# A convolution layer whose weights are split on GpSimd, with its filler products in three reduced-precision parts

## The chip, the cores and the metric

The kernel runs on one core of one Trainium2 chip. The time is the device time of one execution in microseconds (us); it counts as the median over runs. Five engines work beside each other, each through its own fixed list of instructions: TensorE (PE in the profile; its weight loads are PEld), VectorE (DVE), ScalarE (ACT), GpSimd (POOL) and SyncE (SP), which here starts the loads from memory.

## The reference

One step of a trunk of two layers with d = 1024 is computed for 384 columns (tokens): 128 of a sample group (8 streams of 16 tokens) and 256 of a prompt. Each layer has a half-step SwiGLU, a mixer, a cross-attention into 256 memory tokens and another half-step SwiGLU. The mixer of layer 0 is the convolution module that the change is about, the mixer of layer 1 a gated DeltaNet.

```python
def conformer_conv_module(h, conv_buf, w_in, b_in, dw, dw_b, ln_g, ln_b, w_out, b_out):
    u = h @ w_in + b_in
    val, gate = jnp.split(u, 2, axis=-1)
    u = val * jax.nn.sigmoid(gate)
    hist = jnp.concatenate([conv_buf.astype(u.dtype), u], axis=1)
    c = causal_depthwise_conv(hist, dw) + dw_b
    c = jax.nn.silu(layer_norm(c, ln_g, ln_b))
    return c @ w_out + b_out, hist[:, -(CONV_W - 1):]
```

`dw` has 31 taps. Apart from the trunk's output, the keys and values of the prompt's memory are outputs too: for each layer, 256 memory rows times a 1024x1024 matrix for the keys and one for the values. They depend on nothing but the inputs, so they can be computed at any time before layer l's cross-attention uses them.

## The kernel before

**Products.** An fp32 matrix product is made from three products in the faster format fp32r: each operand is split into a high part (a cast, ACT, L189) and a low part (the difference, L197), and high times high, high times low and low times high are added up in PSUM. A weight chunk is 128 rows by 1024 columns. `get` (L276) loads it into one of three buffers `raw`, casts it to `whi` and subtracts into `wlo`; both have eight buffers. In the kernel before, all subtractions are VectorE's. `proj` (L725) gets a chunk and multiplies it with the 384 columns of activations `hTh`, `hTl` (24 matmuls). Loads are started by SyncE, stores by GpSimd (L273), and each of these waits in its place in its engine's list.

**Order.** An `Emitter` records all operations, and a `Scheduler` (L304) sorts them once, ahead of time, into one fixed list per engine, on costs that the code states for each operation. The chip doesn't reorder them.

**The convolution stage** (`conv`, L965). The 1024 features are 8 tiles. For each tile c there are two projections (chunks `cg`, `cv`), the gate (`glu`: a sigmoid on ACT, two multiplications on VectorE, stores of the new history on GpSimd), and 31 taps on VectorE (L210: one multiply-add with both inputs in SBUF for each tap; `TENSOR_SCALAR`, L204, for the first). Fifteen of them for the sample tokens are done earlier, in `old_taps` (L946). Tiles are tapped two at a time. Then, over all tiles: the mean of the features by matmuls with a constant matrix `onesd`, the layer norm `ln` for each of three token tiles, and the output product with eight chunks `co`, token tile by token tile (`tokenwise`). It can start on a token tile when its layer norm is done.

**Filler.** The memory's keys and values are 32 pieces (2 layers, 4 heads, keys and values, 2 halves). `kv` (L903) makes a piece with 16 true fp32 matmuls of 128 columns, each of which the profile records as two. The table `KV` says at which place of the program how many pieces are offered to TensorE: 20 of them in the convolution's stage, between the projections and the mean, while VectorE is at the taps. Whatever is left when a cross-attention needs it is made ahead of it.

**GpSimd before.** It makes small statistics of the norms (`stat`, 128x1 to 128x6), some copies in DeltaNet, memsets and all stores. In the convolution's stage it has memsets and stores.

Of the kernel before, what the change touches and what calls it, by code (L numbers as in the profile page):

```python
# [8 lines left out]
F32 = mybir.dt.float32  # L9
F32R = mybir.dt.float32r  # L10
AF = mybir.ActivationFunctionType
ALU = mybir.AluOpType
# [39 lines left out]

# columns of the per-feature table
# [5 lines left out]
# constant matrices: causal blocks, block sums, decay masks, block-doubling masks  # L59
# [8 lines left out]
def chunk_names():  # L68
    names = [("mem", 0), ("mem", 1), ("bout",)]
    for l in range(2):  # L70
        for i in range(2):
            for f in range(FF):
                names += [("g", l, i, f), ("u", l, i, f), ("d", l, i, f)]
            names += [(n, l, i, j) for n in ("g4", "u4") for j in range(4)]
        names += [("q4", l, 0, j) for j in range(4)]
        for k in range(KT):
            names += [("wq", l, k), ("wo", l, k), ("wk", l, k // 2, k % 2), ("wv", l, k // 2, k % 2)]
# [16 lines left out]
class Emitter:  # L94
    """Records the program in issue order. Tasks beside the main stream are advanced by running
    clocks of the engines, so that their matmuls fall where their operands are ready."""
# [153 lines left out]
    def quad(self, mms):  # L250
        """Products into four groups of 32 rows, which the tensor engine works on at once."""
# [24 lines left out]
    def get(self, name, dest=None):  # L276
        """The two parts of a weight chunk: loaded and split as early as their room is free."""
# [9 lines left out]
        self.tt(lo, raw, hi.bitcast(F32), ALU.subtract)  # L287
# [16 lines left out]
class Scheduler:  # L304
    """Orders the recorded program: a list schedule by the longest way to the end, on the engines'
    known costs, that keeps every dependence between the operations."""
# [8 lines left out]
    def cell(self, ap):  # L315
        """(what, bits): the tile and the columns in it that an operand covers."""
# [123 lines left out]
class Region:  # L440
    """First-fit allocation of the columns of one tile."""
# [5 lines left out]
    def take(self, n, keep=0, high=False):  # L447
# [13 lines left out]
        # of the places at an edge of a hole, the one whose columns were freed the longest ago  # L461
# [19 lines left out]
class Model:  # L481
    def __init__(self, nc, tc, A, O, s, ps):
# [41 lines left out]
    def alloc(self, n, keep=0):  # L524
        """(columns, handle) for the main stream."""
# [19 lines left out]
    def _bank(self):  # L545
# [3 lines left out]
        # the one that has been free for longest  # L549
# [38 lines left out]
    def rows(self, kind, i):  # L588
        """A row of gains on all partitions."""
# [4 lines left out]
    def rstd(self, s1, s2, dep):  # L594
        """(s1 + s2) ** -0.5."""
# [6 lines left out]
    def chain(self, t, y, yb, gpost, gpre, half=False, cross=False):  # L602
        """x += post(y); the next sublayer's normalized input, transposed and split."""
# [79 lines left out]
    def first_chunks(self, names, chains, split):  # L683
# [12 lines left out]
        res = []  # L696
# [1093 lines left out]
```

## Time and profile before

| | |
|---|---|
| median of 3 runs | 1893.7 us (1892.61 to 1894.55) |
| span of the profiled execution | 1891.9 us, 1.8 us below that median |
| projections of the convolution on TensorE, fp32 pieces between them | 312.6 to 397 us |
| fp32 pieces alone | 397 to 454 us |
| taps (after `old_taps`) | 324.2 to 454.2 us |
| mean and layer norm | 454.2 to 477 us |
| first matmul of the output product | 477.0 us |

The profile is one execution. A row such as `L197 DVE TENSOR_TENSOR wlo<-raw,whi 128x1024 fp32r<-128x1024 f32 x361 | 438.1, 1221 | 570.7 <-ACT whi L189 542.7` reads: line 197, engine VectorE, the operation, its output and inputs with their shape, 361 times; 438.1 us busy in all, 1221 ns each; VectorE was idle for 570.7 us just ahead of these, most of it waiting for ACT's cast of line 189. In the timeline a row has its start and its length, both in us. A row of windows has the stretch, its length, and the busy time and number of instructions of each engine.

### The profile page before, as it was taken

To read this page: it belongs to the slowest core of one execution; us is meant where nothing else is said; L and a number is where in the kernel's file an instruction comes from. 1 tells how busy PE (TensorE), PEld (TensorE's weight loads), DVE (VectorE), ACT (ScalarE), POOL (GpSimd) and SP (SyncE) were. 2 spreads that over 40 slices of the span, in tenths; PEclk is the share of its full clock that TensorE was granted. 3 is DMA by queue.
4 is the path that set the end of the run, shared out by engine and by line. 5 is a ranking of instruction groups with operands and counts; after the bars stand their busy time and mean duration, and the time that the engine had idled before them with its cause. 6 is when DMAs were issued, how large, how long until landed. Compare 5 with 4: busy or idle time off the path is not lost.

```text
span 1891.9 us, 27912 instructions
## 1 busy us (share of the span) xinstructions
PE 1870.6 (99%) x10863; PEld 1682.6 (89%) x10863; DVE 1025.5 (54%) x1940; ACT 794.5 (42%) x1589; POOL 168.8 (9%) x407
## 2 busy tenths in 40 slices
PE   8999999999999999999999999999999999999998
PEld 7999999999877899999899999989898767899997
DVE  6564436998653633334633344788886734533333
ACT  4333334312643533233433233787786533433332
POOL 1000002111100100000100000323321101000000
PEclk9999999999999999999999999999999999999999
DMA  8544434556685443434533343433324782444431
GB/s 300 179 136 125 134 112 121 128 147 216 219 312 210 156 129 128 134 123 130 163 122 117 120 134 101 128 97 99 123 90 124 236 311 101 134 134 134 122 123 45
DMA packets 88469, 278.83 MB, mean 147 GB/s; under 512 B 18001, under 2 KB 20561, under 8 KB 88337
## 3 DMA queue, kind: packets, MB, share of 16 engines
q1 hardware_dynamic: 86080, 271.42, 44.7%
q0 software_dynamic: 2256, 5.64, 0.9%
q8 instruction: 85, 1.39, 0.3%
q14 instruction: 48, 0.39, 0.1%
HBM read 265.09 MB, written 11.92 MB: 146 GB/s over the span
## 4 chain that ended last, share of the span: by engine, by line
PE 97%; ACT 1%; DMA 1%; DVE 0%; POOL 0%; issue 0%; SPq 0%; DVEq 0%; POOLq 0%; ACTq 0%
PE ps L247 91%; PE ps L266 3%; PE ps L259 2%; DMA raw<-in_w 0%; POOL stat L197 0%; ACT big L190 0%; DMA x<-in_x 0%; DVE big L210 0%; ACT whi L189 0%; SPq L270 0%; ACT big L189 0%; ACT hTl L190 0%; ACT L190 0%; DVE big L197 0%; DVE wlo L197 0%
## 5 line engine op out<-in xcount | busy, mean ns | idle before, releaser
L197 DVE TENSOR_TENSOR wlo<-raw,whi 128x1024 fp32r<-128x1024 f32 x361 | 438.1, 1221 | 570.7 <-ACT whi L189 542.7
L189 ACT CAST whi<-raw 128x1024 fp32r<-128x1024 f32 x361 | 374.5, 1050 | 640.3 <-PE ps L247 584.6
L247 PE MATMUL ps<-hTh,wlo 128*128 128x384 f32 x1680 | 498.3, 341 | 0.0
L247 PE MATMUL ps<-hTl,whi 128*128 128x384 f32 x1680 | 497.1, 342 | 0.0
L247 PE MATMUL ps<-hTh,whi 128*128 128x384 f32 (+1 forms) x1680 | 496.9, 342 | 0.0
L247 PEld LDWEIGHTS ps<-hTl,whi 128*128 128x128 f32 x1680 | 308.9, 188 | 8.0 <-issue 2.1
L247 PEld LDWEIGHTS ps<-hTh,whi 128*128 128x128 f32 x1680 | 308.8, 188 | 7.9 <-issue 1.2
L247 PE MATMUL ps<-big 128*128 128x128 f32 (+5 forms) x1944 | 308.0, 288 | 7.1 <-DMA big<-in_w 6.7
L247 PEld LDWEIGHTS ps<-hTh,wlo 128*128 128x128 f32 x1680 | 308.7, 188 | 6.5 <-issue 2.3
L247 PEld LDWEIGHTS ps<-big 128*128 128x128 f32 (+1 forms) x1944 | 269.6, 190 | 40.3 <-issue 20.8
L247 PE MATMUL ps<-whi,rbh 128*128 128x512 f32 x672 | 206.0, 396 | 0.4 <-ACT big L189 0.4
L247 PE MATMUL ps<-wlo,rbh 128*128 128x512 f32 x672 | 203.8, 395 | 0.0
L247 PE MATMUL ps<-whi,rbl 128*128 128x512 f32 x672 | 202.5, 393 | 0.0
L210 DVE SCALAR_TENSOR_TENSOR big<-big,cols 128x384 f32<-128x384 f32 (+13 forms) x424 | 189.5, 497 | 2.2 <-ACT big L190 0.3
L247 PEld LDWEIGHTS ps<-whi,rbl 128*128 128x128 f32 x672 | 125.7, 188 | 24.7 <-issue 0.4
L247 PEld LDWEIGHTS ps<-wlo,rbh 128*128 128x128 f32 x672 | 125.3, 188 | 24.6 <-issue 0.4
L247 PEld LDWEIGHTS ps<-whi,rbh 128*128 128x128 f32 x672 | 124.8, 188 | 21.1 <-ACT big L189 0.6
L197 DVE TENSOR_TENSOR big<-big,ps 128x64 f32<-128x64 f32 (+4 forms) x219 | 86.4, 405 | 39.8 <-PE ps L247 39.2
L266 PE MATMUL ps<-ident,big 128*128 128x128 f32 x479 | 89.5, 279 | 5.5 <-DVE big L210 5.4
L247 PE MATMUL ps<-whi,hTh 128*128 128x512 f32 x240 | 87.2, 399 | 0.7 <-ACT hTh L189 0.7
L189 ACT COPY big<-ps 32x32 f32<-32x32 f32 (+5 forms) x155 | 49.6, 324 | 90.2 <-PE ps L247 64.3
L247 PE MATMUL ps<-whi,hTl 128*128 128x512 f32 x240 | 86.3, 398 | 0.0
(82 smaller groups left out, 1350.7 us busy)
## 6 DMA issues: line engine op xcount, KB each, us to landing
raw<-in_w SPq DMA_DIRECT2D x362, 512.0 KB, 3.8
big<-in_w SPq DMA_DIRECT2D x37, 512.0 KB, 5.1
big<-in_ck SPq DMA_DIRECT2D x32, 512.0 KB, 6.5
big<-in_cv SPq DMA_DIRECT2D x32, 512.0 KB, 6.3
big<-in_npre SPq DMA_DIRECT2D x8, 512.0 KB, 7.5
out_pkv<-big POOLq DMA_DIRECT2D x32, 128.0 KB, 5.0
big<-in_npost SPq DMA_DIRECT2D x8, 512.0 KB, 7.3
big<-out_pkv SPq DMA_DIRECT2D x8, 512.0 KB, 5.1
```

What stands on the lines that cost most here:

```text
L189: return self._on("A", cost, dep, lambda: sc.copy(out, in_), [in_], w)
L197: return self._on(eng, cost, dep, lambda: e.tensor_tensor(out=out, in0=a, in1=b, op=op), [a, b], [out])
L210: lambda: v.scalar_tensor_tensor(out=out, in0=a, scalar=s, in1=b, op0=op0, op1=op1), [a, s, b], [out])
L247: self._add("P", cost, lambda: t.matmul(out, lhsT, rhs, start=start, stop=stop, **kw), [lhsT, rhs], [out])
L259: t.matmul(out, lhsT, rhs, start=start, stop=stop)
L266: self._add("P", 109.0, lambda: t.transpose(out, in_, ident), [in_, ident], [out])
```

## The change

The low parts of all weights that the convolution layer uses are made on GpSimd: `get` takes the engine as an argument. These are the sixteen projection chunks, the eight chunks of the output product, its bias, and 20 chunks of the memory products below: 45 subtractions of 128x1024.

The 20 filler pieces in the convolution become three-part products (`kv_split`): all values, as 16 chunks of 256 rows by 512 columns (192 matmuls of 512 columns), and two key pieces (48 matmuls of 256 columns). The memory itself is loaded and split for them into `rbh`, `rbl`. The other 14 key pieces stay true fp32 products in their old places, with 8 matmuls of 256 columns in place of 16 of 128; since the queue holds just the keys now, two of them are left for DeltaNet's place in the table.

The sum over features for the mean is begun on GpSimd: `total` adds the first six tiles (five additions of 128x384), and the mean takes three matmuls, of `total` and the last two tiles, in place of eight. The chunks of keys on chip at the start are 3, not 4. Comments are gone; the lines of `Emitter` keep their numbers.

```diff
-    def get(self, name, dest=None):
+    def get(self, name, dest=None, eng="V"):
...
-        self.tt(lo, raw, hi.bitcast(F32), ALU.subtract)
+        self.tt(lo, raw, hi.bitcast(F32), ALU.subtract, eng=eng)
...
-SLOTS = 4               # chunks of keys and values on chip at the start
+SLOTS = 3
...
-KV = {"start": 3, "f00": 3, "conv": 20, "co": 3, "xo": 0, "f01": 1, "f10": 2, "dn": 6, "f11": 0}
+KV = {"start": 3, "f00": 3, "conv": 2, "co": 3, "xo": 0, "f01": 1, "f10": 2, "dn": 6, "f11": 0}
...
-        self.kvq = [(k, l, h, i) for l in range(2) for h in range(XH) for k in ("wk", "wv") for i in range(2)]
+        self.kvq = [("wk", l, h, i) for l in range(2) for h in range(XH) for i in range(2)]
...
+    def kv_split(self, keys):
...
+        for i in range(2):
+            c = slice(i * D, (i + 1) * D)
+            E.get(("mem", i), dest=(mh[:, c], ml[:, c]), eng="G")
...
+        for l in range(2):
+            for u in range(2):
...
+                for q in range(4):
+                    j, wh, wl = E.get(("v4", l, u, q), eng="G")
+                    for k in range(2 * q, 2 * q + 2):
+                        s = slice(512 * (k % 2), 512 * (k % 2) + 512)
+                        for m in range(2):
+                            c = slice(m * P, (m + 1) * P)
+                            E.mm(o[m], mh[:, k, c], wh[:, s], k == 0, False)
+                            E.mm(o[m], mh[:, k, c], wl[:, s], False, False)
+                            E.mm(o[m], ml[:, k, c], wh[:, s], False, k == KT - 1)
...
+        for _ in range(keys):
...
+            _, l, h, i = self.kvq.pop()
+            j, wh, wl = E.get(("wk", l, h, i), eng="G")
+            o, b = self.bank()
+            self.gmm(o[:, 0:MEM], wh, wl, 0, MEM, mh, ml)
...
-            for m in range(2):
-                c = slice(m * P, (m + 1) * P)
-                for k in range(KT):
-                    a, b_ = (w[:, k, :], mem[:, k, c]) if kind == "wk" else (mem[:, k, c], w[:, k, :])
-                    E.mm(o[:, c], a, b_, k == 0, k == KT - 1)
+            for k in range(KT):
+                E.mm(o[:, 0:MEM], w[:, k, :], mem[:, k, :], k == 0, k == KT - 1)
...
-                    E.mm(mean[:, 0:NTOK], self.onesd, cO[:, c, :], c == 0, c == KT - 1)
...
+                if c0 == 0:
+                    E.tt(total, cO[:, 0, :], cO[:, 1, :], ALU.add, dep=e, eng="G")
+                elif c0 < KT - 2:
+                    for c in cs:
+                        E.tt(total, total, cO[:, c, :], ALU.add, dep=e, eng="G")
+                else:
+                    E.mm(mean[:, 0:NTOK], self.onesd, total, True, False)
+                    for c in cs:
+                        E.mm(mean[:, 0:NTOK], self.onesd, cO[:, c, :], False, c == KT - 1)
...
-                og, bg, eg = self.proj(("cg", c))
-                ov, bv, ev = self.proj(("cv", c))
+                og, bg, eg = self.proj(("cg", c), "G")
+                ov, bv, ev = self.proj(("cv", c), "G")
...
-        self.kv(KV["conv"])
+        self.kv_split(KV["conv"])
...
-        jb, bh, bl = E.get(("bout",), dest=bo)
+        jb, bh, bl = E.get(("bout",), dest=bo, eng="G")
...
-        held = [E.get(("co", k)) for k in range(KT)]
+        held = [E.get(("co", k), eng="G") for k in range(KT)]
```

The scheduler makes new lists of this. On GpSimd, at the taps of the middle tiles, there stood the stores of history (`pconv`, `sconv`), of memory pieces (`pkv`) and a memset:

```order
L273 DMA out_pkv<-big 128x2x128 x2
L273 DMA out_pkv<-big 128x256
L273 DMA out_pconv<-big 128x30
L236 MEMSET big 128x30
L273 DMA out_sconv<-big 1024x1x30
L273 DMA out_pkv<-big 128x256
```

Now the subtractions stand among the history's stores, and after the last of these fifteen follow one another, up to the first addition of `total`:

```order
L197 TENSOR_TENSOR wlo_82<-raw_86,whi_74 128x1024
L197 TENSOR_TENSOR wlo_83<-raw_87,whi_75 128x1024
L197 TENSOR_TENSOR wlo_84<-raw_88,whi_76 128x1024
L273 DMA out_pconv<-big 128x30 x2
L273 DMA out_sconv<-big 1024x1x30
L273 DMA out_pconv<-big 128x30
L197 TENSOR_TENSOR wlo_85<-raw_86,whi_77 128x1024
L197 TENSOR_TENSOR wlo_78<-raw_87,whi_70 128x1024
```

So three subtractions stand ahead of stores that wait for a glu, and the rest behind them. Of the 45, eight stand among the statistics of the feed-forward sublayer ahead of the convolution, and 36 after the first tap.

On VectorE, at the second and third tile's glu (the operations that read `ps`), the list before had subtractions between the taps:

```order
L210 SCALAR_TENSOR_TENSOR big_95<-big_95,cols_92 128x235
L197 TENSOR_TENSOR wlo2_80<-raw2_88,whi2_72 128x1024
L210 SCALAR_TENSOR_TENSOR big_95<-ps5_101,cols_92,big_95 128x256
L210 SCALAR_TENSOR_TENSOR big_95<-big_95,cols_92 128x236
L204 TENSOR_SCALAR big_95<-big_95,cols_92 128x256
```

In the list after, the first two tiles' glu stand close together ahead of the taps, and no subtraction between them:

```order
L210 SCALAR_TENSOR_TENSOR big_95<-ps5_101,cols_92,big_95 128x256
L210 SCALAR_TENSOR_TENSOR big_95<-ps5_101,cols_92,big_95 128x8x16
L204 TENSOR_SCALAR big_95<-big_95,cols_92 128x256
L210 SCALAR_TENSOR_TENSOR big_95<-big_95,cols_92 128x227
L210 SCALAR_TENSOR_TENSOR big_95<-big_95,cols_92 128x228
L210 SCALAR_TENSOR_TENSOR big_95<-ps7_103,cols_92,big_95 128x256
L210 SCALAR_TENSOR_TENSOR big_95<-ps7_103,cols_92,big_95 128x8x16
```

On TensorE, behind the last projection, the value chunks begin (each of `whi`, `wlo`, `rbh` and `rbl` a part of a weight or of the memory), where the fp32 pieces `ps<-big 128x128` had stood:

```order
L247 MATMUL ps6_102<-hTh_66,wlo3_81 128x384
L247 MATMUL ps7_103<-whi4_74,rbh_68 128x512
L247 MATMUL ps7_103<-wlo4_82,rbh_68 128x512
L247 MATMUL ps7_103<-whi4_74,rbl_69 128x512
L247 MATMUL ps7_103<-whi4_74,rbh_68 128x512
```

Four projections are interleaved after the first, so that 94 projection matmuls stand ahead of the end of the second tile's chunks. The mean's three matmuls stand behind all value chunks and both keys:

```order
L247 MATMUL ps7_103<-rbh_68,wlo4_82 128x256
L247 MATMUL ps4_100<-big_95 128x384 x3
L247 MATMUL ps5_101<-big_95 128x256 x8
```

More of the change, by code (lines that the diff above doesn't have):

```diff
@@ L76, in chunk_names @@
         for k in range(KT):
-            names += [("wq", l, k), ("wo", l, k), ("wk", l, k // 2, k % 2), ("wv", l, k // 2, k % 2)]
+            names += [("wq", l, k), ("wo", l, k), ("wk", l, k // 2, k % 2), ("v4", l, k // 4, k % 4)]
     for k in range(KT):
@@ L681, in dmm, with first_chunks @@
             E.pump()
-    def first_chunks(self, names, chains, split):
+    def first_chunks(self, names, chains, split, eng="V"):
         E = self.E
@@ L689, in first_chunks @@
         for n in names[:split]:
-            j, hi, lo = E.get(n)
+            j, hi, lo = E.get(n, eng=eng)
             o, b = self.bank()
@@ L700, in first_chunks @@
             res.append((o, b, e))
-        return res + [self.proj(n) for n in names[split:]]
+        return res + [self.proj(n, eng) for n in names[split:]]
     def wide(self, o, w, t):
@@ L723, in turn, with proj @@
         return o.rearrange("p (k c) -> p k c", k=4), e
-    def proj(self, name):
-        j, hi, lo = self.E.get(name)
+    def proj(self, name, eng="V"):
+        j, hi, lo = self.E.get(name, eng=eng)
         o, b = self.bank()
@@ L879, in kv_open, with result @@
         return True
+    def kv_split(self, keys):
+        E = self.E
+        vt = E.vt
+        mh, ml = (a.rearrange("p k c -> p (k c)")[:, 0:2 * D] for a in (self.rbh, self.rbl))
+        for i in range(2):
+            c = slice(i * D, (i + 1) * D)
+            E.get(("mem", i), dest=(mh[:, c], ml[:, c]), eng="G")
+        mh, ml = (a.rearrange("p (k m) -> p k m", k=KT) for a in (mh, ml))
+        res, rh = self.alloc(1024)
+        nres = [0]
+        def result(o, n):
+            r = res[:, nres[0] % 2 * 512:nres[0] % 2 * 512 + n]
+            nres[0] += 1
+            E.act(r, o[:, 0:n], dep=0)
+            return r
+        for l in range(2):
+            for u in range(2):
+                (o, b) = self.bank2()
+                for q in range(4):
[7 more added lines that the diff above has]
+                            E.mm(o[m], ml[:, k, c], wh[:, s], False, k == KT - 1)
+                            E.pump()
+                    E.done(j)
+                for m in range(2):
+                    r = result(o[m], 512)
+                    for n in range(2):
+                        E.store(self.O["pkv"][l, 2 * u + n][:, 512 + m * MEM:512 + (m + 1) * MEM],
+                                r[:, n * MEM:(n + 1) * MEM])
+                self.bfree(b)
+        for _ in range(keys):
[3 more added lines that the diff above has]
+            self.gmm(o[:, 0:MEM], wh, wl, 0, MEM, mh, ml)
+            E.done(j)
+            E.store(self.O["pkv"][l, h][:, i * MEM:(i + 1) * MEM], result(o, MEM))
+            self.bfree(b)
+        self.free(rh)
+        E.vt = vt
     def early(self, what, order):
@@ L922, in kv @@
             o, b = self.bank()
-            for m in range(2):
-                c = slice(m * P, (m + 1) * P)
-                for k in range(KT):
-                    a, b_ = (w[:, k, :], mem[:, k, c]) if kind == "wk" else (mem[:, k, c], w[:, k, :])
-                    E.mm(o[:, c], a, b_, k == 0, k == KT - 1)
+            for k in range(KT):
+                E.mm(o[:, 0:MEM], w[:, k, :], mem[:, k, :], k == 0, k == KT - 1)
             E.act(res, o[:, 0:MEM], dep=0)
             self.bfree(b)
-            dst = self.O["pkv"][l, h]
-            if kind == "wk":
-                E.store(dst[:, i * MEM:(i + 1) * MEM], res)
-            else:
-                E.store(dst[:, 512:1024].rearrange("p (m d) -> p m d", m=2)[:, :, i * P:(i + 1) * P],
-                        res.rearrange("p (m d) -> p m d", m=2))
+            E.store(self.O["pkv"][l, h][:, i * MEM:(i + 1) * MEM], res)
             if len(self.kvq) >= self.kvslots:
@@ L998, in taps @@
         def taps():
+            total, th = yield from self.galloc(NTOK)
             for c0 in range(0, KT, 2):
@@ L1021, in taps @@
                     self.free(hist[c][1], hist[c][3])
-                    E.mm(mean[:, 0:NTOK], self.onesd, cO[:, c, :], c == 0, c == KT - 1)
+                if c0 == 0:
[7 more added lines that the diff above has]
+                        E.mm(mean[:, 0:NTOK], self.onesd, cO[:, c, :], False, c == KT - 1)
+                    self.free(th)
             self.conv_end = e
@@ L1030, in conv @@
             if c == 0:
-                (og, bg, eg), (ov, bv, ev) = self.first_chunks([("cg", c), ("cv", c)], chains, SPLIT["conv"])
+                (og, bg, eg), (ov, bv, ev) = self.first_chunks([("cg", c), ("cv", c)], chains, SPLIT["conv"], "G")
             else:
-                og, bg, eg = self.proj(("cg", c))
-                ov, bv, ev = self.proj(("cv", c))
+                og, bg, eg = self.proj(("cg", c), "G")
+                ov, bv, ev = self.proj(("cv", c), "G")
             glu(c, og, bg, eg, ov, bv, ev)
@@ L1699, in pack @@
             w[i, 0] = f("ca_b_out")[0]
-        elif t in ("g4", "u4", "q4"):
-            a = wq[n[1]] if t == "q4" else (wg if t == "g4" else wu)[n[1], n[2]]
+        elif t in ("g4", "u4", "q4", "v4"):
+            if t == "v4":
+                a = wv[n[1]][:, n[2] * 512:(n[2] + 1) * 512]
+            else:
+                a = wq[n[1]] if t == "q4" else (wg if t == "g4" else wu)[n[1], n[2]]
             w[i] = a[n[3] * 256:n[3] * 256 + 256, 0:512].reshape(2, P, 512).transpose(1, 0, 2).reshape(P, D)
@@ L1709, in pack @@
             w[i] = g_type(wq[n[1]], n[2] * P)
-        elif t in ("wk", "wv"):
-            w[i] = g_type((wk if t == "wk" else wv)[n[1]], n[2] * MEM + n[3] * P)
+        elif t == "wk":
+            w[i] = g_type(wk[n[1]], n[2] * MEM + n[3] * P)
         elif t == "wo":
```

## The prediction

> **What bounds the kernel now.** The page comes first, for the shares of the engines over the whole span.
>
> ```profile
> span 1891.9 us, 27912 instructions
> PE 1870.6 (99%) x10863; PEld 1682.6 (89%) x10863; DVE 1025.5 (54%) x1940; ACT 794.5 (42%) x1589; POOL 168.8 (9%) x407
> ```
>
> TensorE (PE) is busy 99%, so any matmul saved looks like time saved, and VectorE (DVE) looks idle half the time. But the change lies in the convolution's stage, so I cut the span there. Columns: window, its length, then each engine's busy time, the granted clock, the DMA share and GB/s.
>
> ```profile
> 324.20:397.00 72.80, 72.80 (x475) 72.80 (x475) 69.65 (x157) 19.98 (x30) 14.11 (x24) 1.00 0.51 121
> 397.00:454.30 57.30, 57.30 (x496) 55.98 (x495) 57.06 (x115) 6.21 (x16) 11.04 (x17) 1.00 0.55 167
> 454.30:477.00 22.70, 21.78 (x170) 20.27 (x170) 14.54 (x16) 12.84 (x20) 2.93 (x5) 1.00 0.75 264
> ```
>
> From 324 to 454 us PE is full and DVE is almost full (69.65 of 72.80, 57.06 of 57.30). What DVE does there is the next view, its groups between 324.3 and 454.2, with the timeline's rows of the stage's start and end.
>
> ```profile
> L210 DVE SCALAR_TENSOR_TENSOR big<-big,cols 128x384 f32<-128x384 f32 (+13 forms) x240 | 111.6, 534 | 0.3
> L197 DVE TENSOR_TENSOR wlo<-raw,whi 128x1024 fp32r<-128x1024 f32 x7 | 8.5, 1217 | 0.2 <-ACT whi L189 0.2
> L210 DVE SCALAR_TENSOR_TENSOR big<-ps,cols,big 128x256 f32<-128x256 f32 (+1 forms) x16 | 6.0, 412 | 3.5 <-PE ps L247 2.2 <-ACT big L190 0.7 <-issue 0.5
> L204 DVE TENSOR_SCALAR big<-big,cols 128x256 f32<-128x256 f32 x8 | 3.2, 405 | 0.0
> ...
> 324.24 0.74 DVE L210 SCALAR_TENSOR_TENSOR big<-ps,cols,big 128x256 f32<-128x256 f32 x2 [0.67 <-ACT big L190]
> ...
> 398.21 56.03 DVE L210 SCALAR_TENSOR_TENSOR big<-big,cols 128x238 f32<-128x238 f32 x111
> 454.17 1.21 DVE L197 TENSOR_TENSOR rbl<-raw,rbh 128x1024 fp32r<-128x1024 f32 x1
> ```
>
> Of 130 us, 111.6 are the 240 taps. They end at 454.2, when the first other operation starts, and the mean, the layer norm and the convolution's output product wait for the last of them. PE's memory pieces fill just this time:
>
> ```profile
> 396.98 62.49 PE L247 MATMUL ps<-big 128*128 128x128 f32 x528
> ```
>
> 528 records in 62.49 us are 0.118 us each; a piece of 32 records costs 3.8 us. So the stage has two bounds of nearly one length: PE's list and DVE's taps. To shorten it, both have to shrink.
>
> **The change, part by part.** (1) PE. Twenty pieces of 3.8 us (75.6 us) become 16 value chunks of 12 matmuls 128x512 and two keys of 24 matmuls 128x256. Their steps, from start to start:
>
> ```profile
> 341.06 0.33 PE L247 MATMUL ps<-hTh,whi 128*128 128x384 f32 x1
> ...
> 341.92 0.33 PE L247 MATMUL ps<-hTh,whi 128*128 128x384 f32 x1
> ...
> 483.75 0.39 PE L247 MATMUL ps<-wlo,hTh 128*128 128x512 f32 x1
> ...
> 484.88 0.39 PE L247 MATMUL ps<-whi,hTl 128*128 128x512 f32 x1
> ```
>
> Five steps each: 0.172 us for 384 columns, 0.226 for 512. The values cost 192 x 0.226 = 43.4 us; the two keys, by 0.108 us between these, 48 x 0.113 = 5.4. With a mean of 3 matmuls in place of 8, PE has some 28 us less here. This gain doesn't show, if the taps end later than PE.
>
> (2) DVE's start. The stage begins with a window of projections up to the first glu:
>
> ```profile
> 312.60:324.20 11.60, 11.60 (x71) 11.60 (x70) 3.80 (x5) 4.37 (x5) 0.00 (x0) 1.00 0.46 136
> ```
>
> The first glu now stands behind 94 projection matmuls, since four projections are interleaved: 94 x 0.172 = 16.2 us from 312.6 on, so 329 (with 0.2 for the sigmoid) where it was 324.2: **+4.8**.
>
> (3) DVE's list loses seven subtractions in the taps: **−8.5**, and five in the layer norm that follows:
>
> ```profile
> L197 DVE TENSOR_TENSOR wlo<-raw,whi 128x1024 fp32r<-128x1024 f32 x5 | 6.1, 1218 | 2.2 <-ACT whi L189 2.2
> ...
> 458.76 8.22 DMA raw<-in_w
> ...
> 467.01 1.06 ACT whi L189
> ...
> 468.09 1.23 DVE wlo L197
> 469.31 1.14 DVE big L197
> ```
>
> Only part of those 6.1 us is on the chain (1.23 in its rows, the rest by queueing): **−3**.
>
> (4) GpSimd (POOL). Here lies the price. POOL gets 45 subtractions of 128x1024, 36 of them after the first tap, and five sums of 128x384. No such operation of POOL is in the trace. What the trace has is POOL's small operations beside DVE's (start, length; the first row is the form's usual length, min/median/max in ns):
>
> ```profile
> L197 POOL TENSOR_TENSOR stat<-stat x88: 183/193/1385, 13.2 to 1886.2; 128x1 f32<-128x1 f32 x48, 128x3 f32<-128x3 f32 x40
> ...
> 509.81 1.16 POOL L197 TENSOR_TENSOR stat<-stat 128x1 f32<-128x1 f32 x1 [2.88 <-ACT big L190]
> 515.36 1.20 POOL L197 TENSOR_TENSOR stat<-stat 128x1 f32<-128x1 f32 x1 [2.90 <-ACT hTl L190]
> 1211.82 0.53 POOL L215 COPY big<-big 128x24 f32<-128x24 f32 x1 [0.50 <-DVE big L210]
> ...
> 508.57 2.35 DVE L197 TENSOR_TENSOR wlo<-raw,whi 128x1024 fp32r<-128x1024 f32 x2
> 514.16 2.35 DVE L197 TENSOR_TENSOR wlo<-raw,whi 128x1024 fp32r<-128x1024 f32 x2
> 1211.15 1.13 DVE L210 SCALAR_TENSOR_TENSOR big<-big,cols 128x384 f32<-128x384 f32 x2
> ```
>
> A 0.193 us operation took 1.16 and 1.20 and ended at 510.97 and 516.56, 0.05 us after the DVE pair's end (510.92, 516.51); the copy ended at 1212.35, 0.07 after two operations of the taps' form. So a DVE operation with both inputs in SBUF keeps POOL from reading. Does POOL keep DVE out likewise? These rows speak against a hold for the whole of a POOL instruction:
>
> ```profile
> 1240.72 1.36 POOL L197 TENSOR_TENSOR stat<-stat,negh 128x6 f32<-128x6 f32 x1
> ...
> 1240.82 0.28 DVE L197 TENSOR_TENSOR big<-big 128x128 f32<-128x128 f32 x1
> ...
> 1241.60 1.18 DVE L197 TENSOR_TENSOR wlo<-raw,whi 128x1024 fp32r<-128x1024 f32 x1
> ```
>
> Two DVE operations kept their usual length inside a POOL operation of 1.36 us; but it reads six elements and calculates, where a subtraction reads 2048. I take it that reads exclude each other. The Trainium skill, "SBUF — State Buffer", section "Who interferes with whom", calls the ports that VectorE and GpSimd share an exclusive lock, which a VectorE instruction with two SBUF inputs contends for with any GpSimd instruction that reads SBUF, and which is held for the whole instruction; by that, the taps and POOL's subtractions simply add up. The trace agrees one way (509.81), and not about the whole instruction (1240.72).
>
> The price of a reading element, from the taps' two ends:
>
> ```profile
> L210 DVE SCALAR_TENSOR_TENSOR big<-big,cols 128x384 f32<-128x384 f32 x128 | 70.1, 604 | 0.0
> ...
> L210 DVE SCALAR_TENSOR_TENSOR big<-big,cols 128x227 f32<-128x227 f32 x8 | 3.6, 449 | 0.0
> ```
>
> 155 ns over 157 columns is 0.99 ns a column. POOL, if it reads its two inputs through one port, needs 2 x 1024 x 0.99 = 2.0 us for a subtraction; at least 1.2 (DVE's own, 1217 ns), at most 2.2 (plus the 0.19 of a small one). Of DVE's list, 9.2 of 120.8 us (6.0 from PSUM, 3.2 with one input) leave the port free, 8%: 33 of 36 subtractions cost, 33 x 2.0 = **+66** (40 to 73). The five sums: 5 x 2 x 384 x 0.99 ns = **+3.8**. The Trainium skill, "GPSIMD Engine Reference", section on elementwise work (3.1), measured 4497 ns for a GpSimd addition of 2048 columns; an estimate of 2.25 us by that page would make the first term 74 and the forecast 1970. No run here shows it.
>
> (5) Two of DeltaNet's six filler pieces are new there, in a stretch where PE has no room:
>
> ```profile
> 1180.00:1195.00 15.00, 15.00 (x119) 14.18 (x118) 14.20 (x20) 10.35 (x22) 6.66 (x12) 1.00 0.32 96
> ```
>
> 2 x 3.8 = 7.6; the wider key pieces elsewhere load half as many weights for the same columns, for which I take 2 us off, a choice between nothing and all: **+5.5** (0 to 7.6).
>
> (6) At nothing: ACT's further casts (some 20 of 1.06 us) beside 26 busy us of 130, 21 if that cover went; the transfers (DMA share 0.5); slots and order of the start. Eight subtractions in the tail of the first feed-forward stand between POOL's statistics: 0, at most 6.
>
> Sum: 4.8 − 8.5 − 3 + 66 + 3.8 + 5.5 = +68.6. The profiled span of 1891.9 lies 1.8 under the median of 1893.7; carried over, **1962 us**.
>
> **The rivals.** *POOL reads in the gaps* (0.15). DVE's reads take 0.99 ns of a column, but its operations last longer: the fixed part, 604 − 384 x 0.99 = 224 ns, times 240 taps is 54 us in which its port may be free; if 37 us of it, two thirds (my choice), can be used, the sum falls to +32, **1925**, and with a 1.2 us subtraction 1905. For: the 1240.72 row. Against: POOL waited out pairs of DVE operations whole, without slipping in between.
>
> *DVE always wins* (0.11). POOL gets in only where DVE waits. The taps then end at 329 + 121 = 450, and only after that come the 16 value chunks (43.4) and two keys (5.4) on PE: mean at about 499 instead of 454, +45, and with (3), (5): +48, **1942**. The rows from 509.81 on, where only POOL was held up, speak for it; against it, that DVE was there first in each of them, so that they show no contest.
>
> *POOL costs DVE nothing* (0.20, the other side). The reads don't hinder the taps: 4.8 − 8.5 − 3 + 5.5 = −1.2, **1892.5**, the same as before; with the pieces of (5) hidden 1887, faster. For: 1240.72, and no row shows a DVE operation made longer by POOL. Against: the port rows. It decides at the hold: 1.2 / 33 = 0.04 us for a subtraction; anything above makes the change slower.
>
> *POOL's queue* (0.04). Its stores wait in order:
>
> ```profile
> L273 POOL DMA_DIRECT2D out_pkv<-big x32 | 21.1, 660 | 99.1 <-ACT big L189 98.2 <-DVE big L210 0.5 <-issue 0.4
> ```
>
> POOL stood 98.2 us behind such waits for ACT. Low parts now queue behind stores of the glu's rows, and PE behind the low parts; if PE stands still for 40 us more, over **1995**.
>
> **How the numbers follow.** Adding up: 0.50, gaps 0.15, DVE wins 0.11, nothing 0.20, queue 0.04. The range goes from the lower edge of no change, 1890, to 1995 (the forecast's 73 and the tail's 6 give 1975, and 20 for some of POOL's queue). It leaves out the faster half of the fourth (0.10) and the fifth. The first case's own range is 1936 to 1975. A measurement tells 0.2% (3.8 us) from no change: faster 0.10, same 0.10, slower 0.80.
>
> **What would show it.** Right: taps longer than 604 ns in the mean beside POOL's subtractions, POOL's 128x1024 rows of 2 us and more, ending with DVE's, the last tap near 520, and PE idle in the conv stage, waiting for DVE. Gaps: the same, the last tap near 485. DVE wins: taps of 604 ns, POOL's subtractions after them. Wrong: taps of 604 ns ending near 450 with POOL's subtractions beside them; then the port isn't shared in this direction. Term (5) shows as the time from the conv's output product to the end of the span, against before.

## The result, and the profile after

The changed kernel takes 1998.0 us (median of 4 runs, 1995.7 to 2000.0) where the kernel before takes 1893.9: a ratio of 1.055, 95% interval 1.054 to 1.057. The forecast was 1962 us, its range ended at 1995. The side was right, the size was not: +104 us where the sum had +69.

The page of the profile after begins:

```profile
span 1997.1 us, 26848 instructions
PE 1875.7 (94%) x10293; PEld 1662.8 (83%) x10293; DVE 1054.8 (53%) x1915; ACT 823.0 (41%) x1607; POOL 340.9 (17%) x457
```

TensorE is idle for some 120 us now. One stretch, 312 to 560 us, first in the profile before, then after (columns as in the prediction's windows):

```profile
312.00:560.00 248.00, 246.96 (x1704) 225.50 (x1703) 194.18 (x357) 90.31 (x167) 38.12 (x64) 1.00 0.62 194
```

```profile
312.00:560.00 248.00, 158.43 (x770) 141.16 (x769) 184.79 (x281) 67.66 (x93) 182.37 (x89) 0.82 0.42 114
```

TensorE falls from 247 to 158 busy us, GpSimd rises from 38 to 182 (its rows count the time that an operation is held up, too), and the granted clock falls to 0.82. The landmarks of the stage in the profile after: the first projection, the first tap, a run of taps that ends with the last one (494.91 + 24.95), the first matmul of the output product.

```profile
320.81 0.94 PE L247 MATMUL ps<-hTh,whi 128*128 128x384 f32 x4
...
559.17 0.58 PE L247 MATMUL ps<-whi,hTh 128*128 128x512 f32 x1
```

```profile
340.07 4.98 DVE L210 SCALAR_TENSOR_TENSOR big<-big,cols 128x227 f32<-128x227 f32 x2
...
494.91 24.95 DVE L210 SCALAR_TENSOR_TENSOR big<-big,cols 128x384 f32<-128x384 f32 x47
```

Before, they lay at 312.6, 325.3, 454.2 and 477.0; the rows of the first tap and of the output product are these:

```profile
325.34 0.95 DVE L210 SCALAR_TENSOR_TENSOR big<-big,cols 128x227 f32<-128x227 f32 x2
...
477.04 0.48 PE L247 MATMUL ps<-whi,hTh 128*128 128x512 f32 x1
```

So the stretches grew by 8.2 (to the first projection), 6.5 (to the first tap), 50.9 (the taps, 128.9 to 179.8) and 16.5 us (last tap to output product, 22.8 to 39.3). That is 82; the rest, 23, is lost behind the product.

What VectorE's groups look like between 340 and 520, by form:

```profile
L210 DVE SCALAR_TENSOR_TENSOR big<-big,cols 128x384 f32<-128x384 f32 x128 | 83.9, 709 | 0.0
L210 DVE SCALAR_TENSOR_TENSOR big<-big,cols 128x240 f32<-128x240 f32 x8 | 15.7, 1966 | 0.0
L204 DVE TENSOR_SCALAR big<-big,cols 128x256 f32<-128x256 f32 x8 | 10.2, 1278 | 0.0
...
L210 DVE SCALAR_TENSOR_TENSOR big<-big,cols 128x239 f32<-128x239 f32 x8 | 3.7, 457 | 0.0
...
L210 DVE SCALAR_TENSOR_TENSOR big<-ps,cols,big 128x256 f32<-128x256 f32 x7 | 3.3, 476 | 13.7 <-ACT big L190 10.3 <-PE ps L247 3.4
```

Two neighbours in size, 240 and 239 columns, have means of 1966 and 457 ns: a few of the eight are stretched, the others not at all. Summed over each operation's excess over the shortest of its form, 23 operations are 51.0 us longer. TENSOR_SCALAR, 405 ns before, is among them; the operations that read PSUM are not. In the timeline of GpSimd, then of VectorE, one can see who holds whom:

```profile
367.36 13.81 POOL L197 TENSOR_TENSOR wlo<-raw,whi 128x1024 fp32r<-128x1024 f32 x1 [3.25 <-ACT whi L189]
...
409.60 7.16 POOL L197 TENSOR_TENSOR wlo<-raw,whi 128x1024 fp32r<-128x1024 f32 x3
423.35 14.86 POOL L197 TENSOR_TENSOR wlo<-raw,whi 128x1024 fp32r<-128x1024 f32 x6 [6.58 <-ACT whi L189]
...
495.66 25.05 POOL L197 TENSOR_TENSOR big<-big 128x384 f32<-128x384 f32 x1 [4.85 <-DVE big L210]
520.66 0.57 POOL L273 DMA_DIRECT2D out_pkv<-big  x1
```

```profile
408.34 0.49 DVE L210 SCALAR_TENSOR_TENSOR big<-ps,cols,big 128x256 f32<-128x256 f32 x1 [3.37 <-PE ps L247]
408.74 8.30 DVE L210 SCALAR_TENSOR_TENSOR big<-big,cols 128x240 f32<-128x240 f32 x1
416.96 0.40 DVE L204 TENSOR_SCALAR big<-big,cols 128x256 f32<-128x256 f32 x1
```

At 408.74 one tap takes 8.30 us, until three subtractions that follow one another are done. At 495.66 one addition of 384 columns, about a microsecond of work, takes 25.05 us, until the last 47 taps are done, and the stores behind it wait too. TensorE needs the buffer of such a store:

```profile
503.18 0.39 PE L247 MATMUL ps<-whi,rbl 128*128 128x512 f32 x1
524.09 0.58 PE L247 MATMUL ps<-rbh,whi 128*128 128x256 f32 x1 [20.53 <-ACT big L189]
```

So each of the two engines makes the other wait for whole instructions. Which of them goes next isn't the same everywhere: from 423.56 to 438.46 six subtractions (the row at 423.35) and six operations of VectorE took turns, one by one, each of VectorE's lasting 2.4 to 2.6 us.

The same shows ahead of the stage, in the tail of the feed-forward, where VectorE's updates of the norm have two inputs in SBUF:

```profile
302.41 2.86 DVE L210 SCALAR_TENSOR_TENSOR big<-x,stat,big 128x512 f32<-128x512 f32 x1
```

Such an update takes 0.74 us undisturbed. Four of them ran beside four of GpSimd's subtractions there and are 6.3 us longer together.

My theory after the result: this lock makes all of the 82 us, some directly on VectorE's operations, the rest through GpSimd's list, whose stores and low parts come late. The rival: GpSimd is simply slow (2.4 us for a subtraction), and its long list in fixed order is what everyone waits for.

### The profile page after: what moved, and what is told of

Its sections match the earlier page's. It is cut to its first block, busy times and chain, and to the rows that moved or that the text cites. A ratio compares the mean times of both kernels' runs of the same rounds, so it can differ in the third digit from the quotient of the medians.

```text
span 1997.1 us, 26848 instructions
## 1 busy us (share of the span) xinstructions
PE 1875.7 (94%) x10293; PEld 1662.8 (83%) x10293; DVE 1054.8 (53%) x1915; ACT 823.0 (41%) x1607; POOL 340.9 (17%) x457
## 4 chain that ended last, share of the span: by engine, by line
PE 68%; DVE 2%; DMA 2%; issue 2%; ACT 1%; POOL 1%; POOLq 0%; DVEq 0%; ACTq 0%
PE ps L247 64%; PE ps L266 2%; PE ps L259 2%; DVE big L210 1%; DMA raw<-in_w 1%; DMA out_pkv<-big 1%; ACT whi L189 0%; DVE wlo L197 0%; POOL stat L197 0%; ACT big L190 0%; POOL wlo L197 0%; DMA big<-in_w 0%; ACT hTl L190 0%; DVE x L210 0%; POOL out_pkv L273 0%
## 5 line engine op out<-in xcount | busy, mean ns | idle before, releaser
L197 DVE TENSOR_TENSOR wlo<-raw,whi 128x1024 fp32r<-128x1024 f32 x337 | 408.9, 1221 | 568.4 <-ACT whi L189 471.9
L247 PE MATMUL ps<-hTh,whi 128*128 128x384 f32 x1680 | 528.3, 343 | 23.0 <-ACT big L190 21.4
L247 PE MATMUL ps<-hTl,whi 128*128 128x384 f32 x1680 | 529.6, 341 | 0.0
L247 PE MATMUL ps<-hTh,wlo 128*128 128x384 f32 x1680 | 526.0, 341 | 0.3 <-POOL wlo L197 0.3
L247 PE MATMUL ps<-whi,rbh 128*128 128x512 f32 x736 | 233.8, 402 | 38.4 <-DVE big L210 25.2
L247 PE MATMUL ps<-big 128*128 128x128 f32 (+6 forms) x1134 | 233.9, 318 | 10.1 <-DMA big<-in_w 8.1
L210 DVE SCALAR_TENSOR_TENSOR big<-big,cols 128x384 f32<-128x384 f32 (+11 forms) x424 | 232.0, 600 | 2.1 <-ACT big L190 0.3
L247 PEld LDWEIGHTS ps<-big 128*128 128x128 f32 (+1 forms) x1134 | 183.0, 189 | 47.6 <-issue 17.3
L197 POOL TENSOR_TENSOR wlo<-raw,whi 128x1024 fp32r<-128x1024 f32 x42 | 137.1, 3291 | 104.0 <-ACT whi L189 94.5
L266 PE MATMUL ps<-ident,big 128*128 128x128 f32 x479 | 91.8, 282 | 17.6 <-DVE big L210 16.8
L204 POOL TENSOR_SCALAR stat<-stat 128x1 f32<-128x1 f32 (+2 forms) x48 | 14.4, 301 | 540.6 <-ACT hTl L190 526.0
L215 POOL COPY big<-big 128x24 f32<-128x24 f32 (+2 forms) x96 | 32.6, 360 | 372.3 <-issue 240.6
```

The source lines that it names most:

```text
L197: return self._on(eng, cost, dep, lambda: e.tensor_tensor(out=out, in0=a, in1=b, op=op), [a, b], [out])
L204: return self._on(eng, cost, dep, lambda: e.tensor_scalar(out=out, in0=a, scalar1=s1, scalar2=s2, op0=op0, **kw), [a, s1, s2 if s2 is not ...
L210: lambda: v.scalar_tensor_tensor(out=out, in0=a, scalar=s, in1=b, op0=op0, op1=op1), [a, s, b], [out])
L215: return self._on(eng, cost, dep, lambda: e.tensor_copy(out, in_), [in_], [out])
L247: self._add("P", cost, lambda: t.matmul(out, lhsT, rhs, start=start, stop=stop, **kw), [lhsT, rhs], [out])
L266: self._add("P", 109.0, lambda: t.transpose(out, in_, ident), [in_, ident], [out])
```

## The experiments

**The port by itself.** Seven trials behind the end of the kernel before, on data that nobody uses: GpSimd alone, VectorE alone, then pairs started together.

```diff
+PROBES = [("stt", 0, "sub", 4), ("stt", 30, "sub", 0), ("stt", 30, "sub", 4), ("sttps", 30, "sub", 4), ("ts", 30, "sub", 4), ("stt", 30, "set", 4), ("stt", 30, "copy", 4)]
```

> The kernel before with seven short trials after its end, on data of its own: GpSimd alone, VectorE alone, then 30 operations of VectorE (three forms) beside four of GpSimd (three forms), each pair started together. Lock: 30 taps with two SBUF inputs keep their length, and GpSimd's subtraction of 2.4 us ends with the last of them, or one tap is held for all of GpSimd's four, 9 us; taps with one input from PSUM don't touch the four subtractions; a GpSimd memset touches nothing; a copy of GpSimd behaves like the subtraction; TENSOR_SCALAR with one SBUF input contends, as it did in the changed kernel (1.82 and 2.40 us in place of 0.40). Sharing (the two take turns element by element): each of the overlapping operations gets longer by a part, none waits for a whole one of the other side.

GpSimd's four operations in the trials with taps, with taps that read PSUM, with TENSOR_SCALAR, with memsets in place of subtractions, and with copies:

```profile
1917.52 10.55 POOL L1800 TENSOR_TENSOR raw<-big 128x1024 f32<-128x1024 f32 x4
...
1945.47 9.63 POOL L1800 TENSOR_TENSOR raw<-big 128x1024 f32<-128x1024 f32 x4
...
1965.55 9.83 POOL L1800 TENSOR_TENSOR raw<-big 128x1024 f32<-128x1024 f32 x4
...
1989.12 3.98 POOL L1802 MEMSET raw<- 128x1024 f32 x4
...
2009.24 3.22 POOL L1804 COPY raw<-big 128x384 f32<-128x384 f32 x4
```

VectorE in the trial with taps and in the trial with PSUM:

```profile
1917.42 13.02 DVE L1791 SCALAR_TENSOR_TENSOR raw<-raw,cols,raw 128x384 f32<-128x384 f32 x8
```

```profile
1945.37 11.06 DVE L1793 SCALAR_TENSOR_TENSOR raw<-ps,cols,raw 128x384 f32<-128x384 f32 x17
```

In 11.06 us stand 17 taps that read PSUM, 0.65 us each, and four subtractions beside them took 9.63. With both inputs in SBUF the time of 13.02 us held 8 taps: four of them lasted 2.58 us, one for each subtraction. Four TENSOR_SCALAR lasted 2.38 us (0.48 once GpSimd was done), taps beside the copies 0.74 (0.62 once they were done), the memsets held no tap. So for the taps it is a lock on reading, held for whole instructions. One thing was not as expected: neither side was shut out for long. In the trial each tap depends on the one before, and 0.04 us lie between them; GpSimd got in there each time. In the kernel two tiles' taps alternate, and the next overlaps the one before (47 taps of 0.6 us in 24.95). That this is the difference isn't shown: the operations that took turns from 423.56 on overlap as well.

**The lock in its place, with nothing else changed.** Sixteen subtractions of 128x720 that nobody uses, among the taps of the kernel before; in the second kernel memsets in the same places. The lists of TensorE and VectorE are those of the kernel before in both.

```diff
+                    if j % 8 == 5:
+                        h = hist[cs[j // 8 % 2]][0]
+                        E.tt(idle, h[:, :, 0:30], idle.bitcast(F32), ALU.subtract, dep=e, eng="G")
```

> The kernel before with sixteen subtractions of 128x720 on GpSimd that nobody uses, spread over the taps; the lists of TensorE and VectorE are word for word those of before. Lock: each holds a tap or is held by an unbroken stretch of taps; some 1.7 us each, the last tap 15 to 27 us later at 470 to 480, and stores behind a held subtraction may stop TensorE; 1905 to 1925 us. Rival (GpSimd's reads cost VectorE nothing): 1890 to 1897 us.

> The same with sixteen memsets of 128x720 in the subtractions' places in GpSimd's list (they write and read nothing). Lock on reading: no tap is longer, the last tap at 454; 1890 to 1897 us. Rival (it is GpSimd's list, its length and what stands behind what, that costs): the same time as with the subtractions.

With subtractions 1954.6 us, ratio 1.033 (1.031 to 1.034); with memsets 1894.3, ratio 1.001 (1.000 to 1.002). The rival falls: GpSimd's operations in the same order cost next to nothing when they don't read. The memsets are shorter (0.72 us, a subtraction of this size 1.59 where nothing holds it), but the difference, 14 us over all sixteen, is not what 61 us come from. Memsets aren't free of the lock either: two TENSOR_SCALAR beside them were 1.5 us longer together, the taps not at all. The forecast by the lock was too small, though, for the second effect. GpSimd, then TensorE, in the kernel with subtractions:

```profile
415.78 59.39 POOL L197 TENSOR_TENSOR rbl<-big,rbl 128x720 fp32r<-128x720 f32 x1
475.12 0.74 POOL L273 DMA_DIRECT2D out_pkv<-big  x1
```

```profile
477.93 2.08 PE L247 MATMUL ps<-big 128*128 128x128 f32 x8 [33.11 <-ACT big L189]
```

A subtraction of 1.6 us took 59.39 us here: it stood behind an unbroken run of taps and two subtractions of VectorE. TensorE filled the two result buffers, and stood still for 33.11 us until the store behind the subtraction went. The last tap came only 17 us later than before (471.5); the rest of the +61 is TensorE's list, full before, which has 52 us of waiting in it when the output product begins (537.9), 33 of them here.

**The lock taken away in the changed kernel.** The taps' sums lie in PSUM, so that a tap has one input in SBUF. GpSimd keeps all it has.

```diff
+                for c in cs:
+                    acc[c] = yield from self.gbank()
+                    E.act(acc[c][0][:, 0:P], cO[:, c, 0:P], dep=dep)
...
-                            o = cO[:, c, P + n:]
+                            o = y[:, P + n:NTOK]
```

> The changed kernel with the taps' sums in PSUM: each tap reads one input from SBUF and one from PSUM, and the last writes to SBUF. GpSimd keeps all its subtractions, additions and stores. Lock: no contention is left, taps of 0.61 us, subtractions of 2.4 us beside them, the last tap near 455 to 465, the output product some 23 us later; 1915 to 1930 us. Rival (GpSimd's pace and its queue are the price): the low parts come as late as before, TensorE still waits, the last tap after 490; 1965 us or more.

1915.6 us, ratio 1.012 (1.011 to 1.014). VectorE's and GpSimd's groups in the stage:

```profile
L210 DVE SCALAR_TENSOR_TENSOR ps<-big,cols,ps 128x384 f32<-128x384 f32 (+14 forms) x232 | 106.2, 542 | 0.1
```

```profile
L197 POOL TENSOR_TENSOR wlo<-raw,whi 128x1024 fp32r<-128x1024 f32 x29 | 69.0, 2396 | 22.7 <-PE ps L247 16.1 <-ACT whi L189 6.3
```

```profile
476.56 0.59 PE L247 MATMUL ps<-whi,hTh 128*128 128x512 f32 x1
```

No tap is stretched, a subtraction takes 2.40 us beside them, the last tap ends at 457.5, and the output product begins at 476.56 where it began at 477.04 before the change and at 559.17 after. In sum all 82 us are gone. The first projection still begins at 320.0, since the updates ahead of it read SBUF twice as before; these 7.4 us are made up by VectorE's list, which has 8.5 us of subtractions less in the taps. A tap on PSUM is no shorter than one on SBUF (542 and 534 ns in the mean), so the gain is the port's. The control for that was the same edit in the kernel before:

> The kernel before with the taps' sums in PSUM and nothing else, as a control for the run of the changed kernel with sums in PSUM. Lock: GpSimd reads next to nothing at the taps, so nothing changes, 1890 to 1898 us, last tap at 454. Rival (taps from PSUM are quicker in themselves, and the changed kernel gained by that): the last tap comes 20 us or more earlier, and the time falls by what TensorE allows.

It took 1943.6 us, ratio 1.027 (1.025 to 1.028), which neither side had expected. The edit brings a wait of its own there: VectorE stood 20.4 us for ACT's copy into the new PSUM buffer, which is less than half of the 49.6 us by which the last tap came later (503.8), and TensorE, whose filler was done by then, waited 40.1 us. As a control it failed; the durations of the taps have to do.

**One part alone.** The kernel before, with only the sixteen projection chunks' low parts on GpSimd.

```diff
+                og, bg, eg = self.proj(("cg", c), "G")
+                ov, bv, ev = self.proj(("cv", c), "G")
```

> The kernel before, with one thing of the change: the low parts of the convolution's sixteen projection chunks on GpSimd. Filler, mean and the rest as before. Lock: some nine of the sixteen fall beside taps, each holds VectorE for 2.4 us where it saves 1.2, and GpSimd's operations wait in VectorE's unbroken stretches, so that projections come late; with 5 to 8 us in the tail of the feed-forward ahead: 1905 to 1930 us. Rival (no price on VectorE): VectorE's list is 8.5 us shorter, 1885 to 1893 us.

1915.8 us, ratio 1.012 (1.010 to 1.013): in the range that the lock gave, and not the rival's. In the taps five operations of VectorE were stretched by 11.4 us, and one subtraction took 14.4. But of the 22 us only 5.5 lie between the first projection and the output product; 8.7 lie ahead of it (the first projection at 321.3), and 7.9 behind, where TensorE had 50 more filler records, 5.6 us, to do.

**Parts undone.** First all low parts back on VectorE; then the mean by eight matmuls again, without GpSimd's additions; then four result buffers for the split filler in place of two.

```diff
-        self.tt(lo, raw, hi.bitcast(F32), ALU.subtract, eng=eng)
+        self.tt(lo, raw, hi.bitcast(F32), ALU.subtract)
```

> The changed kernel with all 45 low parts on VectorE again; the split filler and the sums on GpSimd stay. Theory (the port is a lock, held for whole instructions, by GpSimd as well as by VectorE): the 51 us by which 23 operations of VectorE were stretched go, and 36 subtractions of 1.22 us come into VectorE's list, 44 us; the taps end near 490 to 500 and not 520, no tap longer than 0.61 us except beside an addition of the sum; 1940 us, 1925 to 1960. Rival (the port costs little, GpSimd's slow list with its waiting stores kept TensorE and VectorE waiting): without subtractions in that list the stage falls back to what VectorE's list gives too, but the stretched operations stay wherever GpSimd adds; 1940 us as well, so this run sizes the way back and does not part the two.

```diff
-                    E.mm(mean[:, 0:NTOK], self.onesd, total, True, False)
+                for c in cs:
+                    E.mm(mean[:, 0:NTOK], self.onesd, cO[:, c, :], c == 0, c == KT - 1)
```

> The changed kernel without the five additions on GpSimd; the mean takes eight matmuls, as before the change. Theory (the addition that stood 25 us behind the taps held up the stores and low parts behind it, and so the mean, the layer norm and the product): from the last tap to the output product 25 us and not 39; about 1984 us. Rival (whatever stands there starves: the next subtraction waits for the end of the taps in the addition's place, and the stores behind it): 1998 us, within 5.

```diff
-        res, rh = self.alloc(1024)
+        res, rh = self.alloc(2048)
```

> The changed kernel with four buffers for the results of the split filler in place of two. Theory (between the last tap and the mean TensorE waits for results whose stores stand in GpSimd's list behind the addition that the taps keep out): the waits for ACT's copies, 39 us in all, shrink by 15 to 25 us; the mean still waits for the additions, which follow the end of the taps; 1985 to 1995 us. Rival (only the additions and low parts count): 1998 us, within 4.

The first took 1949.2 us (ratio 1.030, 1.028 to 1.031), the last tap at 484.2: 49 us less than the change, but VectorE's list is too long then. As expected, this run doesn't part the two theories. Its first projection begins at 312.5, as before the change. The second took 1998.4 (1.056, 1.054 to 1.058), nothing gained. Its timeline of GpSimd shows why:

```profile
476.83 37.11 POOL L197 TENSOR_TENSOR wlo<-raw,whi 128x1024 fp32r<-128x1024 f32 x1
513.88 2.15 POOL L273 DMA_DIRECT2D out_pkv<-big  x4
```

A subtraction stood in the addition's place and took 37.11 us, with the stores behind it. The theory that I had written down for this run fell, its rival held: whatever reads there is shut out. The third took 1986.5 (1.050, 1.048 to 1.051), 11.5 less, as forecast; but the waits for results shrank only from 39.1 to 36.1 us, not by 15 to 25, and the gain came as a last tap 4.7 us earlier and 5.4 us less from it to the output product. Two more buffers don't reach over a wait of this length.

**What is lost behind the convolution.** Two key pieces are made in DeltaNet's place that were made in the convolution before. This run leaves their matmuls out, so that those keys are not computed.

```diff
-        self.kv(KV["dn"])
+        self.kv(KV["dn"], False)
```

> The changed kernel without the matmuls of the two key pieces that are left for DeltaNet's place (their outputs hold other numbers; loads, copies and stores stay). Theory (these two are TensorE's time in a stretch where it has no room): 7.5 us less than the changed kernel, 1988 to 1992 us, all of it behind the fourth feed-forward. Rival (they fill waits there, and what the program loses behind the convolution comes from another order of its lists): within 3 us of 1998.

1987.6 us (1.050, 1.049 to 1.052), 10.4 less than the change: the two pieces cost about the 7.6 us of their matmuls or somewhat more.

**A better version was tried for and not found.** With sums in PSUM, TensorE has idle time in the stage; two runs moved the other filler there, one of them and a third put the first four low parts on VectorE.

```diff
-KV = {"start": 3, "f00": 3, "conv": 2, "co": 3, "xo": 0, "f01": 1, "f10": 2, "dn": 6, "f11": 0}
+KV = {"start": 3, "f00": 3, "conv": 7, "co": 3, "xo": 0, "f01": 0, "f10": 0, "dn": 0, "f11": 0}
```

> The changed kernel with sums in PSUM, and seven split keys in the convolution in place of two, so that no filler is left for the two feed-forwards behind it and DeltaNet (3 and 2 pieces). Theory (VectorE's taps set the stage; TensorE stands idle there for some 18 us, so what the cheaper filler saved shows only if other pieces are moved in): five pieces of 2.9 us fit there and five of 3.8 us vanish elsewhere: 1896 to 1902 us. Rival (the fillers elsewhere covered waits, or GpSimd's list is full): 1908 us or more.

> The same, with the low parts of the first two tiles' projections (four chunks) on VectorE, as before the change. Theory (in the tail of the feed-forward the statistics of GpSimd and the updates of VectorE wait for these subtractions): the first projection begins at 312 to 315 us and not at 320; 5 to 8 us less than the run with seven keys, 1889 to 1896 us. Rival (the tail is longer for another cause): the same time as that run.

> The changed kernel with sums in PSUM, and the low parts of the first two tiles' projections (four chunks) on VectorE. Theory (the tail of the feed-forward is longer because GpSimd's statistics and VectorE's updates wait for subtractions): the first projection at 312 to 316 us in place of 320, the last tap as much earlier; 1905 to 1911 us. Rival (the tail is longer because of the order of TensorE's list): 1916 us, within 4.

The first two took 1934.0 and 1935.4 us (1.021 and 1.022). The table rewrites the scheduler's lists from their start, and in the first feed-forward, which the edit doesn't touch, TensorE now waited 12.4 us for VectorE (16 times) in the first run and 15.7 us for ACT (14 times) in the second, where it hardly waits for either without the edit; so they say nothing of their theories. The third took 1914.2 (1.012), within the scatter of the 1915.6 without its edit. The first projection began at 316.6 in place of 320.0, so these four chunks make 3.4 of the 7.4 us there; the product came 4.8 us earlier, of which the medians show 1.4.

## Why the prediction was right or wrong

| term of the sum | predicted | measured |
|---|---|---|
| tail of the feed-forward ahead | 0, at most 6 | +8.2 |
| first glu, first tap | +4.8 | +6.5 |
| taps, first to last | −8.5 + 66 | +50.9 |
| additions, layer norm | +3.8 − 3 | +16.5 |
| behind the output product | +5.5 | +23.1 |

- **What bounds the stage** was right: VectorE's taps. TensorE's saving of 28 us shows nowhere; with sums in PSUM, where nothing else is in the way, the product begins half a microsecond earlier than before, and TensorE waits.
- **The start** was right for the first glu (5.0 us in place of 4.8, beside the tail's shift). The other 1.5 us are a TENSOR_SCALAR that a subtraction stretched.
- **The tail ahead**, put at nothing, cost 8.2 us. The prediction placed GpSimd's eight subtractions there between its statistics only; they also stretched VectorE's updates, by 6.3 us. It is the lock once more, on operations that the sum didn't count.
- **The price on the taps** was right in mechanism and 15 us too large in its term: 51.0 us of stretching in place of 66, and 10 us more idle time of VectorE, which I hadn't. GpSimd's subtraction takes 2.4 us, not the 2.0 that I derived; but it is not priced 33 times, because part of them ran in VectorE's waits or after the last tap. The exception that I made for TENSOR_SCALAR was wrong.
- **The step that failed** is the one that priced the lock only as time of VectorE. I wrote that the rivals "DVE always wins" and "POOL's queue" were other cases with 0.11 and 0.04. They are the other half of the same case: an unbroken run of taps can shut GpSimd out (an addition of 1 us took 25 here, a subtraction of 1.6 us 59 in the run with idle subtractions), the stores and low parts in its list stand behind the one that is shut out, and TensorE and the mean behind those. This makes the +16.5 after the taps. The sum had the additions' bare time in that place, 3.8 us, less 3 for VectorE's shorter list. With the taps in PSUM, and the same list on GpSimd, this stretch is 19.1 us, shorter than before the change.
- **Behind the product** lies the largest miss, 17.6 us. The term was the two pieces, 5.5 us where their run gave 10.4; the 2 us that wider pieces were to save aren't there (16 records in 3.72 us at 540.91, where a piece took 3.8). The other 13 or so us stand in other places: in the tail of the cross-attention and of DeltaNet TensorE waits some 3 and 5 us for VectorE's updates in lists that the scheduler wrote in another order; some 5 us are placed by no view. The run with sums in PSUM has them too (22 us behind the product), and so has the run with all low parts on VectorE (19), so the lock at the taps isn't their cause; the run with idle subtractions, whose lists are those of before, has not. That an order is their cause is argued, not shown.
- **The rival on the other side**, that GpSimd's reads cost VectorE nothing, leaned on the row at 1240.72. That operation reads six elements; it could not tell.
- **A slip in the rivals:** gaps with a 1.2 us subtraction add up to 1899, not 1905.
- **The Trainium skill**, "SBUF — State Buffer", section "Who interferes with whom", has, for VectorE's modes that use two ports, the lock held for a whole instruction by whoever issues first, and the other fully blocked. The trace agrees both ways for single instructions with two SBUF inputs (a tap took 2.58 us beside a subtraction, a statistic of GpSimd 1.16 at 509.81); that an addition stood out 47 taps in a row (25.05 us) is more than this. It also says that `tensor_scalar` can enter a mode that uses the shared ports: the trace agrees, 2.38 us in place of 0.48. In the prediction I had set the whole-instruction part aside on one row.
- **The Trainium skill**, "GPSIMD Engine Reference", section 3.1: the estimate of 2.25 us from its figure against 2.35 to 2.40 measured; the row-based 2.0 was further off.

## What to carry to other kernels

Before work goes to GpSimd, look at what VectorE does at that time: if its operations have two SBUF inputs (or are TENSOR_SCALAR on SBUF, as some are here), a reading GpSimd operation doesn't run beside them. It holds one of them up for its whole length, or, where they follow one another without a gap, it can be held until their run ends, and every store in GpSimd's list waits with it. Price such an exclusion from both sides, and name who consumes what the locked-out engine's list holds. For these taps an input in PSUM took the lock away, at next to no cost in the operation's length; the copies into PSUM can bring waits of their own, as they did in the kernel before.

## What the runs showed that I had not expected

- Who goes next isn't settled. In the trial a gap of 0.04 us between taps was enough for GpSimd to get in; in the kernels overlapping taps kept it out for most of 59.39 us, or took turns with it (423.56 to 438.46), and three subtractions in a row kept a tap out until 8.30 us had gone. In the changed kernel six operations of GpSimd came into a run of taps after a pause of more than 1 us; each waited until VectorE came to an operation that reads PSUM, or until the run ended. One that came after 0.53 us (460.25) got in behind the tap that was running. No run tests what decides.
- Two of TensorE's waits cost more than their length. After the 4.42 us wait at 532.94 the same matmuls of 256 columns started every 0.21 us, and from 537.34 on every 0.12:

```profile
532.94 0.58 PE L247 MATMUL ps<-rbh,whi 128*128 128x256 f32 x1 [4.42 <-ACT big L189]
533.32 0.41 PE L247 MATMUL ps<-rbl,whi 128*128 128x256 f32 x1
533.53 0.41 PE L247 MATMUL ps<-rbh,wlo 128*128 128x256 f32 x1
...
537.34 0.28 PE L247 MATMUL ps<-rbh,wlo 128*128 128x256 f32 x1
537.46 0.28 PE L247 MATMUL ps<-rbh,whi 128*128 128x256 f32 x1
```

The granted clock (the third number from the end) was 0.50 in the first of these stretches and 1.00 in the second; before the change it was 1.00 throughout the stage:

```profile
533.00:537.00 4.00, 4.00 (x19) 4.00 (x20) 0.00 (x0) 1.04 (x1) 3.88 (x7) 0.50 0.76 234
537.30:540.00 2.70, 2.62 (x12) 1.48 (x10) 0.00 (x0) 2.10 (x3) 0.06 (x1) 1.00 0.19 35
```

After the 20.53 us wait at 524.09 it went the same way: steps of 0.21 us up to 526.82, then 0.12.
